# Weight ring of a two-layer mixture-of-experts trunk: single-slot transfers for the first eight experts, and norm rows loaded as 2 KB pieces and spread by products with ones

## The chip, the cores and the metric

The kernel runs on one core of a Trainium2 chip. The metric is the device time of one execution in microseconds (us), as the median of several runs; a profile of one execution gives the trace.

## The reference, cut to what matters

Two layers, each an attention block ("mixing") followed by a routed feed-forward block over 32 experts. 256 tokens of width 1024; each token goes to 2 experts, and every expert's three matrices (w1 and w3 together 4 MB, w2 2 MB, in float32) are read once per layer. Two norms per layer have a scale row g and an offset row b.

```python
h = layer_norm(x, ln_in_g, ln_in_b)
for l in range(DEPTH):                                   # 2
    mix = mixing_sublayer(h, ...)
    h = layer_norm(DEEPNORM_ALPHA * h + mix, ln1_g[l], ln1_b[l])
    ffn = hierarchical_moe(h, ...)                       # sum over chosen experts of
                                                         # gate * (silu(x @ w1[e]) * (x @ w3[e])) @ w2[e]
    h = layer_norm(DEEPNORM_ALPHA * h + ffn, ln2_g[l], ln2_b[l])
```

## The kernel before, in words

**The ring of weight slots.** All large weights pass through 1 MB slots (128 partitions x 2048 floats). `Ring` (L141) holds them as tiles of two slots and, some, of one. `jobs` (L270 to L332) lists every transfer in the order of use, with its size of one or two slots. `fill` (L180) hands the next job to a place that is free: a job of two slots needs both halves of one tile, and a job of one slot takes a lone slot first (`fits`, L171). `free` (L197) returns slots when the last matmul that reads them stands in the program. This happens while the program is built, so it fixes which transfer waits for which matmul. SP issues all these transfers on one queue, strictly in the order of the list: a transfer whose slot is still being read stops those behind it. During the experts there are 22 slots: eight tiles of two, and six lone slots.

**Experts.** `up_parts` and `down_parts` (L112, L117) say in how many pieces an expert's up weights (w1 and w3) and down weights (w2) come. Before, with `FINE = 6`, experts 0 to 5 bring their up weights in four pieces of one slot, experts 0 to 3 their down weights in two; the others come in pieces of two slots, up to the last two experts. Experts are worked off in 16 pairs i (L1513). For each pair TensorE does `up_proj` of its first expert (L1394, 32 matmuls), the down products `y_part` of the pair before (L1418, py then px), `up_proj` of its second expert, and `combine` of the pair before into four accumulators (L1430); then `scatter` (L1377, written to px), the transposes T of `glu` (L1227) and, for every second i, a `gather` (L1338). TensorE's order is written by hand (`manual_schedule`, L1512). py, px, T and ph are single PSUM banks.

**The norm rows.** The residual x*g + b of the norm before is added in two steps: `next(residual)` at i = 2 and i = 3 (L1533 to L1537). Two lone jobs of the list after pair 2, "gb" and "x", take the two halves of one tile. `gb_rows` (L265) loads the 8 KB row of g and b into "gb", read 128 times so that each partition has it: 1 MB. `residual_ffn` (L1305) scales it by ALPHA on ScalarE (L1309), computes x*g + b in "x" on GpSimd (L1313 to L1316) and at i = 3 adds it to the accumulators with four matmuls (L1320), after which both slots are freed. In the last layer one more 1 MB job "gb" stands at the end of the list (L331), for the output norm (L1564 to L1578).

Of the kernel before, what the change touches and what calls it, by code (L numbers as in the profile page):

```python
# [9 lines left out]
F32 = mybir.dt.float32  # L10
I32 = mybir.dt.int32
AF = mybir.ActivationFunctionType
# [3 lines left out]
L, S, D = 2, 256, 1024  # L16
# [6 lines left out]
ALPHA = (2 * L) ** 0.25  # L23
# [1 line left out]
NEG = -1e30  # L25
F32R = mybir.dt.float32r
SCRATCH = 1024
LIT, FINE = 3, 6
RING, PRE, LATE, EARLY, LATER = 4, 2, 6, 1, 4
STAGE, GT = 4, 2  # L30
ORDER = (2, 3, 0, 1)
# [80 lines left out]
def up_parts(e):  # L112

    return 4 if e < FINE or e >= NE - 2 else 2


def down_parts(e):  # L117

    return 2 if e < FINE - 2 else 1


def rsqrt(nc, pool, v, n):
# [81 lines left out]
def program(tc, I, out):  # L204
    nc = tc.nc
# [10 lines left out]
    def bcast(src, n):  # L216
        return bass.AP(tensor=src.tensor, offset=src.offset, ap=[[0, 128], [1, n]])
# [30 lines left out]
    ones = const.tile([128, 128], F32, name="ones")  # L248
# [13 lines left out]
                                  bass.AP(tensor=src.tensor, offset=src.offset + at + m * i, ap=[[n, 128], [1, m]]))  # L262
        return job

    def gb_rows(i):  # L265
        def job(t):
            nc.sync.dma_start(t, bcast(I["lnrows"][i], 2 * D))
        return job

    jobs = []  # L270
    for l in range(L):
        at = 0
        for key, size in mixing_plan():
            jobs.append(((l, *key), whole(wmix[l], at, size, 2 if key == ("m",) else 1), 2))
            at += 128 * size

        def up(e):

            flat = wup[l, e].rearrange("p k s f -> p (k s f)")
            parts = up_parts(e)  # L280
            n = 8192 // parts

            def job(i):
                return lambda t: nc.sync.dma_start(t[:, :n], flat[:, n * i:n * i + n])
            return [((l, "up", e, i), job(i), 4 // parts) for i in range(parts)]

        def down(e):
            flat = wdown[l, e].rearrange("p a j f -> p (a j f)")
            parts = down_parts(e)
            n = 4096 // parts  # L290

            def job(i):
                return lambda t: nc.sync.dma_start(t[:, :n], flat[:, n * i:n * i + n])
            return [((l, "w2", e, i), job(i), 2 // parts) for i in range(parts)]

        def last(es):

            held = []

            def rows(t, e, j):  # L300
                nc.sync.dma_start(t.rearrange("p (a j f) -> p a j f", a=2, j=4)[:, :, 2 * j:2 * j + 2],
                                  wdown[l, e][:, :, 2 * j:2 * j + 2])

            def first(t):
                held.append(t)
                rows(t, es[0], 0)

            def second(t):
                rows(t, es[1], 0)
                rows(held[0], es[0], 1)  # L310
                rows(t, es[1], 1)

            return [((l, "w2", e, 0), job, 2) for e, job in zip(es, (first, second))]

        n = NE // 2
        for i in range(n):
            if i in APART:
                jobs += [job for both in zip(up(2 * i), up(2 * i + 1)) for job in both]
            else:
                jobs += up(2 * i)  # L320
                jobs += down(2 * i - 2) + down(2 * i - 1) + up(2 * i + 1)
            if i == n - 2:
                jobs += down(2 * i) + down(2 * i + 1)
            if i == n - 1:
                jobs += last((2 * i, 2 * i + 1))
            if i == 2:
                jobs += [((l, "gb"), gb_rows(1 + 2 * l), 1), ((l, "x"), lambda t: None, 1)]
            if i == 5:
                jobs += [((l, "over", 0), lambda t: None, 2), ((l, "over", 1), lambda t: None, 1)]
        if l == L - 1:  # L330
            jobs += [((l, "gb"), gb_rows(2 + 2 * l), 1)]  # L331
    jobs = [(key, size, job) for key, job, size in jobs]  # L332
    early = {l: next(j for j in jobs if j[0] == (l, "up", 0, 3)) for l in range(L)}
    ring = Ring([j for j in jobs if j not in early.values()], nc.sync)
# [798 lines left out]
    def experts(l, lg, logits, split, late, c2, acc, two_parts):  # L1133
        nonlocal h
        p1 = c2.enter_context(pool_(name=f"moe{l}", bufs=1))
        wkp = c2.enter_context(pool_(name=f"wk{l}", bufs=1, space=PS, side="right"))
# [161 lines left out]
        def affine_T(xg, px, k0):  # L1298
# [3 lines left out]
                last = nc.vector.tensor_scalar(xg[:, k0 + k], px[:, k], g, b, op0=OP.mult, op1=OP.add)  # L1302
            return last

        def residual_ffn():  # L1305

            gb = ring[(l, "gb")].rearrange("p (j a d) -> p j a d", j=2, a=2)
            x = ring[(l, "x")].rearrange("p (t a d) -> p t a d", t=2, a=2)
            nc.scalar.activation(gb, gb, AF.Copy, scale=ALPHA)  # L1309
            for t in range(2):  # L1310
                xv = ring[(l, "x")][:, D * t:D * t + D]
                xv = xv.rearrange("q (p k) -> q k p", k=8) if l == L - 1 else xv.rearrange("q (k p) -> q k p", k=8)
                nc.gpsimd.tensor_tensor(xv, two_parts[0][:, t].bitcast(F32), two_parts[1][:, t].bitcast(F32), op=OP.add)  # L1313
                for a in range(2):
                    nc.gpsimd.tensor_tensor(x[:, t, a], x[:, t, a], gb[:, 0, a], op=OP.mult)
                    nc.gpsimd.tensor_tensor(x[:, t, a], x[:, t, a], gb[:, 1, a], op=OP.add)  # L1316
            yield
            for t in range(2):
                for a in range(2):
                    nc.tensor.matmul(acc[t][a], ident, x[:, t, a], start=False, stop=False, skip_group_check=True)  # L1320
            ring.free((l, "gb"), (l, "x"))
            yield
# [189 lines left out]
        with tc.manual_schedule(engines={mybir.EngineType.PE}):  # L1512
            for i in range(n - 1):  # L1513
                if i:
                    hs = up(i, 0)
                    if i - 1 in APART:
                        down_both(i - 1)
                    else:
                        for a in range(2):
                            y_part(i - 1, a)  # L1520
                    glu(i, 0, hs)
                    hs = up(i, 1)
                if i % 2:
                    q = (i + 1) // 2
                    Dm[q] = p1.tile([128, 2, 4 * C], F32R, name="Dm")
                    placed(q, 0, 1)
                Dg = (gated_both if i + 1 in APART else gated)(i + 1)
                if i:
                    if i - 1 in APART:
                        combine_both(i - 1)  # L1530
                    else:
                        combine(i - 1, *every)
                if i == 2:  # L1533
                    residual = residual_ffn()
                    next(residual)
                if i == 3:
                    next(residual)  # L1537
                scatter(i + 1, Dg)
                if i % 2:
                    for _ in gather(q):  # L1540
                        pass
                if i:
                    glu(i, 1, hs)
                if 4 <= i < 7:
                    found = next(listing)
                if i == 7:
                    overflow(*found)
                    ring.free((l, "over", 0), (l, "over", 1))
            for a in range(2):
                y_part(n - 2, a)  # L1550
            hs = evacuated(up_both(n - 1))
            combine(n - 2, *every)
            glu_both(n - 1, hs)
            down_both(n - 1)
            combine_both(n - 1)
            if l < L - 1:
                warm(wkp.tile([128, 128], F32, name="py"), 16)
        ms = moments(sts)
        h = rows()
        if l < L - 1:  # L1560
            for t in range(2):
                norm(t, acc[t], ms[t])
        else:
            gb = ring[(l, "gb")].rearrange("p (j a d) -> p j a d", j=2, a=2)  # L1564
            for t, (mean, y, nm) in enumerate(ms):
                less = small.tile([128, 1], F32, name="less")
                nc.vector.tensor_scalar(less, mean, -1.0, None, op0=OP.mult)
                for a in range(2):
                    x = halves(t)[a]
                    if t < a:  # L1570
                        nc.vector.scalar_tensor_tensor(x, acc[t][a], mean, gb[:, 0, a], op0=OP.subtract, op1=OP.mult)
                    else:
                        nc.scalar.activation(x, acc[t][a], AF.Identity, bias=less)
                        nc.gpsimd.tensor_tensor(x, x, gb[:, 0, a], op=OP.mult)
            for t, (mean, y, nm) in enumerate(ms):
                for a in range(2):
                    x = halves(t)[a]
                    nc.vector.scalar_tensor_tensor(x, x, y, gb[:, 1, a], op0=OP.mult, op1=OP.add)  # L1578
                    (nc.scalar if a else nc.sync).dma_start(out[128 * t:128 * t + 128, 512 * a:512 * a + 512], x)
# [5 lines left out]
    for l in range(L):  # L1585
        experts(l, *mixing(l))
# [57 lines left out]
```

## Time and profile before

| what | value |
|---|---|
| median of 3 runs | 1424.08 us (1423.87 to 1425.05) |
| the profiled execution | 1425.94 us, its span 1424.3 us |
| TensorE matmul busy | 1346.2 us (95% of the span) |
| VectorE, ScalarE, GpSimd busy | 579.0, 435.1, 86.6 us |
| moved by DMA | 488.69 MB |
| mean granted TensorE clock | 0.983 |

Layer 0 is mixing up to about 270 us and experts up to about 704 us; layer 1 is mixing up to about 974 us and experts up to about 1408 us. Busy shares are averages over stages with different limits: the DMA engines are near full only in the experts, where TensorE is near full as well, so what a change is worth is read from the waits in that stage.

### The profile page before, as it was taken

To read this page: it belongs to the slowest core of one execution; us is meant where nothing else is said; L and a number is where in the kernel's file an instruction comes from. 1 tells how busy PE (TensorE), PEld (TensorE's weight loads), DVE (VectorE), ACT (ScalarE), POOL (GpSimd) and SP (SyncE) were. 2 spreads that over 40 slices of the span, in tenths; PEclk is the share of its full clock that TensorE was granted. 3 is DMA by queue.
4 is the path that set the end of the run, shared out by engine and by line. 5 is a ranking of instruction groups with operands and counts; after the bars stand their busy time and mean duration, and the time that the engine had idled before them with its cause. 6 is when DMAs were issued, how large, how long until landed. Compare 5 with 4: busy or idle time off the path is not lost. (4 is left out here: it accounts for less than half of the span.)

```text
span 1424.3 us, 19771 instructions
## 1 busy us (share of the span) xinstructions
PE 1346.2 (95%) x8004; PEld 832.7 (58%) x8008; DVE 579.0 (41%) x1387; ACT 435.1 (31%) x906; POOL 86.6 (6%) x83
## 2 busy tenths in 40 slices
PE   8999999899999999989789999998999999999893
PEld 8999999543443443434379999984443434434331
DVE  6767777621221221212267676865211212112113
ACT  5556555321111111111145665543211111111111
POOL 2000030130000000000100000301300000000001
PEclk9999999999999999999999999999999999999998
DMA  9433577699999999999963337777999999999995
GB/s 387 189 119 134 214 318 300 252 398 420 427 433 424 429 429 429 431 428 427 425 257 126 119 127 301 308 282 292 390 429 430 430 425 429 430 428 431 428 425 222
DMA packets 46832, 488.69 MB, mean 343 GB/s; under 512 B 4880, under 2 KB 8464, under 8 KB 12816
## 3 DMA queue, kind: packets, MB, share of 16 engines
q1 hardware_dynamic: 46016, 486.25, 82.4%
q8 instruction: 65, 1.06, 0.3%
q10 hardware_dynamic: 720, 1.12, 0.2%
q14 instruction: 31, 0.25, 0.0%
HBM read 486.31 MB, written 1.05 MB: 342 GB/s over the span
## 5 line engine op out<-in xcount | busy, mean ns | idle before, releaser
L1394 PE MATMUL ph<-wslot,xg 128*64 128x512 f32 x1792 | 396.9, 595 | 2.6 <-ACTq L1236 2.6
L1394 PEld LDWEIGHTS ph<-wslot,xg 128*64 128x64 f32 x1792 | 123.7, 137 | 235.1 <-issue 231.6
L479 DVE TENSOR_TENSOR split<-wslot,split 128x512 fp32r<-128x512 f32 (+1 forms) x272 | 192.6, 719 | 96.1 <-ACT split L478 62.7
L478 ACT ACTIVATE split<-wslot 128x512 fp32r<-128x512 f32 (+2 forms) x276 | 168.8, 616 | 140.7 <-PE mm L510 120.2
L508 PE MATMUL mm<-hThi,split 128*128 128x256 f32 x704 | 202.5, 288 | 0.0
L510 PE MATMUL mm<-hThi,split 128*128 128x256 f32 x704 | 197.7, 281 | 0.3
L509 PE MATMUL mm<-hTlo,split 128*128 128x256 f32 x704 | 196.9, 280 | 0.0
L1220 ACT ACTIVATE hs<-ph 128x512 f32<-128x512 f32 x60 | 35.9, 598 | 404.9 <-PE ph L1394 373.1
L1422 DVE SCALAR_TENSOR_TENSOR ys<-py,gate,ys 128x512 fp32r<-128x512 f32 x28 | 21.0, 750 | 286.1 <-ACT ys L1421 286.1
L508 PEld LDWEIGHTS mm<-hThi,split 128*128 128x128 f32 x704 | 132.5, 188 | 3.7 <-ACT split L478 1.3
L510 PEld LDWEIGHTS mm<-hThi,split 128*128 128x128 f32 x704 | 132.3, 188 | 2.5 <-DVE split L479 2.3
L509 PEld LDWEIGHTS mm<-hTlo,split 128*128 128x128 f32 x704 | 132.5, 188 | 0.5 <-issue 0.5
L1418 PE MATMUL py<-wslot,gT 128*64 128x512 f32 x448 | 113.4, 614 | 9.9 <-DMA wslot<-in_down_dram 9.4
L1418 PE MATMUL px<-wslot,gT 128*64 128x512 f32 x448 | 107.8, 592 | 0.0
L1380 DVE TENSOR_SCALAR DT<-px 128x256 fp32r<-128x256 f32 x30 | 12.7, 424 | 218.2 <-PE px L1377 218.2
L1418 PEld LDWEIGHTS py<-wslot,gT 128*64 128x64 f32 x448 | 36.0, 141 | 80.6 <-issue 75.7
L1418 PEld LDWEIGHTS px<-wslot,gT 128*64 128x64 f32 x448 | 36.3, 137 | 62.5 <-issue 62.5
L1430 PE MATMUL acc<-ys,DT 128*128 128x512 f32 x224 | 59.7, 408 | 0.0
L1430 PEld LDWEIGHTS acc<-ys,DT 128*128 128x128 f32 x224 | 39.9, 188 | 30.3 <-issue 22.8
L1422 DVE SCALAR_TENSOR_TENSOR ys<-px,gate,ys 128x512 fp32r<-128x512 f32 x28 | 21.0, 751 | 75.5 <-ACT ys L1421 75.5
L1421 ACT ACTIVATE ys<-py,gate 128x512 fp32r<-128x512 f32 x28 | 19.3, 688 | 102.2 <-PE py L1418 102.2
L1421 ACT ACTIVATE ys<-px,gate 128x512 fp32r<-128x512 f32 x28 | 19.3, 688 | 77.3 <-PE px L1418 77.3
(330 smaller groups left out, 1802.4 us busy)
## 6 DMA issues: line engine op xcount, KB each, us to landing
wslot<-in_up_dram SPq DMA_DIRECT2D x96, 2048.0 KB, 17.9
wslot<-in_down_dram SPq DMA_DIRECT2D x52, 2048.0 KB, 18.9
wslot<-in_wmix_dram SPq DMA_DIRECT2D x32, 2048.0 KB, 8.7
wslot<-in_up_dram SPq DMA_DIRECT2D x64, 1024.0 KB, 14.2
wslot<-in_down_dram SPq DMA_DIRECT2D x24, 1024.0 KB, 10.9
wslot<-in_wmix_dram SPq DMA_DIRECT2D x4, 832.0 KB, 12.9
wslot<-in_lnrows_dram SPq DMA_DIRECT2D x3, 1024.0 KB, 15.4
wslot<-in_wmix_dram SPq DMA_DIRECT2D x2, 1040.0 KB, 11.5
```

The source lines that it names most:

```text
L478: nc.scalar.activation(hi, w, AF.Copy)
L479: engine.tensor_tensor(lo, w, hi.bitcast(F32), op=OP.subtract)
L508: nc.tensor.matmul(ps, st[0], mv[0], start=start, stop=False)
L509: nc.tensor.matmul(ps, st[0], mv[1], start=False, stop=False)
L510: nc.tensor.matmul(ps, st[1], mv[0], start=False, stop=stop)
L1220: nc.scalar.activation(hs, hps.rearrange("q (p j) -> q j p", j=4), AF.Copy)
L1380: nc.vector.tensor_scalar(DT, pd, 0.0, None, op0=OP.is_gt)
L1394: nc.tensor.matmul(ph[C * s:C * s + C], x[:, k, c0:c0 + C], w[:, k % part, s], start=k == 0, stop=k == 7)
L1418: nc.tensor.matmul(py[C * e:C * e + C], gTs[i, e][:, j], w[:, 0 if parts == 2 else a, j], start=j == 0, stop=j == 3)
L1421: nc.scalar.activation(ys[0], py, AF.Copy, scale=gate)
L1422: nc.vector.scalar_tensor_tensor(ys[1], py, gate, ys[0].bitcast(F32), op0=OP.mult, op1=OP.subtract)
L1430: nc.tensor.matmul(acc[t][a], st[i]["DT"][:, t], y, start=False, stop=False, skip_group_check=True)
```

## The change

`FINE` is 8, and `down_parts` uses the same bound: the up weights of experts 6 and 7 come in four pieces instead of two, the down weights of experts 4 to 7 in two instead of one, 8 transfers more per layer for the same bytes. The three 1 MB loads of norm rows become four loads of 512 floats each (2 KB, 8 KB together) into partitions 0, 32, 64 and 96 of the slot "x", and a new function `spread` copies them to all partitions: for each quarter a product of one row of ones (1 x 128) with the row (1 x 512) into py or px, and an ACTIVATE that writes it, scaled, into "gb". It stands at i = 2 of both layers. For the output norm a pair of jobs "gb2" and "x2" stands after pair 9 of the last layer instead of the job at the list's end, spread at i = 11; "gb2" is held until the end.

```diff
-LIT, FINE = 3, 6
+LIT, FINE = 3, 8
...
-    return 2 if e < FINE - 2 else 1
+    return 2 if e < FINE else 1
...
-    def gb_rows(i):
+    def rows_of(i):
+
         def job(t):
-            nc.sync.dma_start(t, bcast(I["lnrows"][i], 2 * D))
+            for j in range(4):
+                nc.sync.dma_start(t[32 * j:32 * j + 1, 0:512], I["lnrows"][i, 512 * j:512 * j + 512])
         return job
...
-                jobs += [((l, "gb"), gb_rows(1 + 2 * l), 1), ((l, "x"), lambda t: None, 1)]
+                jobs += [((l, "gb"), lambda t: None, 1), ((l, "x"), rows_of(1 + 2 * l), 1)]
...
-        if l == L - 1:
-            jobs += [((l, "gb"), gb_rows(2 + 2 * l), 1)]
+            if i == 9 and l == L - 1:
+                jobs += [((l, "gb2"), lambda t: None, 1), ((l, "x2"), rows_of(2 + 2 * l), 1)]
...
+        def spread(key, rows, scale):
+
+            for j in range(4):
+                ps = wkp.tile([128, 512], F32, name=("py", "px")[j % 2])
+                p = slice(32 * j, 32 * j + 1)
+                nc.tensor.matmul(ps, ones[p], ring[(l, rows)][p, 0:512], start=True, stop=True)
+                nc.scalar.activation(ring[(l, key)][:, 512 * j:512 * j + 512], ps, AF.Copy, scale=scale)
+
         def residual_ffn():
 
+            spread("gb", "x", ALPHA)
             gb = ring[(l, "gb")].rearrange("p (j a d) -> p j a d", j=2, a=2)
             x = ring[(l, "x")].rearrange("p (t a d) -> p t a d", t=2, a=2)
-            nc.scalar.activation(gb, gb, AF.Copy, scale=ALPHA)
...
+                if i == 11 and l == L - 1:
+                    spread("gb2", "x2", 1.0)
+                    ring.free((l, "x2"))
...
-            gb = ring[(l, "gb")].rearrange("p (j a d) -> p j a d", j=2, a=2)
+            gb = ring[(l, "gb2")].rearrange("p (j a d) -> p j a d", j=2, a=2)
```

The transfers of experts 5 to 7 on SP's queue in layer 0, before (in_up is up weights, in_down is down weights; 128x4096 fills two slots; the slot tiles' numbers are kept):

```order
L284 DMA wslot0_78<-in_up_dram 128x2048 x2
L267 DMA wslot1_182<-in_lnrows_dram 128x2048
L284 DMA wslot2_190<-in_up_dram 128x4096
L284 DMA wslot5_2100<-in_up_dram 128x4096
L293 DMA wslot6_2101<-in_down_dram 128x4096
L293 DMA wslot7_2102<-in_down_dram 128x4096
L284 DMA wslot3_191<-in_up_dram 128x4096
L284 DMA wslot4_194<-in_up_dram 128x4096
```

And now, in the changed kernel's line numbers:

```order
L286 DMA wslot0_78<-in_up_dram 128x2048 x2
L269 DMA wslot1_182<-in_lnrows_dram 1x512 x4
L286 DMA wslot_2815<-in_up_dram 128x2048
L286 DMA wslot5_2100<-in_up_dram 128x2048
L286 DMA wslot2_190<-in_up_dram 128x2048 x2
L295 DMA wslot5_2100<-in_down_dram 128x2048
L295 DMA wslot6_2101<-in_down_dram 128x2048 x2
L295 DMA wslot9_3070<-in_down_dram 128x2048
L286 DMA wslot10_3071<-in_up_dram 128x2048
L286 DMA wslot11_3072<-in_up_dram 128x2048
L286 DMA wslot12_3073<-in_up_dram 128x2048
L286 DMA wslot7_2102<-in_up_dram 128x2048
```

The up weights of experts 6 and 7 and the down weights of 4 and 5 are cut to single slots, and lone slots (2815, wslot9 to wslot12) are used once more. Further on in the same queue, from the down weights of expert 10 to those of expert 13, before:

```order
L293 DMA wslot1_182<-in_down_dram 128x4096
L293 DMA wslot0_78<-in_down_dram 128x4096
L284 DMA wslot2_190<-in_up_dram 128x4096
L284 DMA wslot5_2100<-in_up_dram 128x4096
L284 DMA wslot6_2101<-in_up_dram 128x4096
L284 DMA wslot3_191<-in_up_dram 128x4096
L293 DMA wslot4_194<-in_down_dram 128x4096
L293 DMA wslot1_182<-in_down_dram 128x4096
```

And now:

```order
L295 DMA wslot1_182<-in_down_dram 128x4096
L295 DMA wslot3_191<-in_down_dram 128x4096
L286 DMA wslot4_194<-in_up_dram 128x4096
L286 DMA wslot7_2102<-in_up_dram 128x4096
L286 DMA wslot0_78<-in_up_dram 128x4096
L286 DMA wslot5_2100<-in_up_dram 128x4096
L295 DMA wslot6_2101<-in_down_dram 128x4096
L295 DMA wslot1_182<-in_down_dram 128x4096
```

Tiles between have other numbers, but here nothing moved against its release: the down weights of expert 13 take, as before, the tile (wslot1) that those of expert 10 leave. On TensorE, at the end of i = 2 in layer 0, before:

```order
L1394 MATMUL ph<-wslot_78,xg 64x512 x8
L1430 MATMUL acc_3006<-ys,DT 128x512 x2
L1430 MATMUL acc_3007<-ys,DT 128x512 x2
L1430 MATMUL acc_3008<-ys,DT 128x512 x2
L1430 MATMUL acc_3009<-ys,DT 128x512 x2
L1377 MATMUL px<-cp,Dg 128x128 x2
L1227 MATMUL T<-cp,hs 128x128 x4
```

And now:

```order
L1404 MATMUL ph<-wslot_78,xg 64x512 x8
L1440 MATMUL acc_3006<-ys,DT 128x512 x2
L1440 MATMUL acc_3007<-ys,DT 128x512 x2
L1440 MATMUL acc_3008<-ys,DT 128x512 x2
L1440 MATMUL acc_3009<-ys,DT 128x512 x2
L1312 MATMUL py<-wslot_182,ones 128x512
L1312 MATMUL px<-wslot_182,ones 128x512
L1312 MATMUL py<-wslot_182,ones 128x512
L1312 MATMUL px<-wslot_182,ones 128x512
L1387 MATMUL px<-cp,Dg 128x128 x2
L1229 MATMUL T<-cp,hs 128x128 x4
```

The four products of `spread` stand ahead of the scatter's transposes, which write px as well.

## Rows read from the trace of the kernel before

**Rows 1.** The page's slices: 40 equal ones of the span, GB/s moved.

```profile
GB/s 387 189 119 134 214 318 300 252 398 420 427 433 424 429 429 429 431 428 427 425 257 126 119 127 301 308 282 292 390 429 430 430 425 429 430 428 431 428 425 222
```

**Rows 2.** Chain that ended last, pieces in time: start us, us, what.

```profile
1321.32 33.84 DMA wslot<-in_down_dram
...
1355.18 29.51 DMA wslot<-in_up_dram
...
1384.75 19.65 DMA wslot<-in_down_dram
...
1406.39 0.02 issue
```

**Rows 3.** TensorE's waits, 600 to 705 us: us, times, longest.

```profile
PE py L1418 <- DMA wslot<-in_down_dram: 5.1, 2, 3.9
```

**Rows 4.** TensorE's timeline: start us, us, instructions [idle before].

```profile
274.87 7.07 PE L1453 MATMUL ph<-wslot,xg 128*32 128x512 f32 x64
...
1383.45 4.83 PE L1453 MATMUL ph<-wslot,xg 128*32 128x512 f32 x36
...
1394.56 1.91 PE L1453 MATMUL ph<-wslot,xg 128*32 128x512 f32 x12 [1.38 <-DMA wslot<-in_up_dram]
```

**Rows 5.** Line L267: duration ns min/median/max, first and last start us.

```profile
L267 SPq DMA_DIRECT2D wslot<-in_lnrows_dram x3: 327/328/4590, 289.4 to 1387.2; - x3
```

**Rows 6.** Stretches: us, then PE PEld DVE ACT POOL busy, PEclk, DMA share, GB/s.

```profile
316.00:318.00 2.00, 2.00 (x12) 0.72 (x10) 0.00 (x0) 0.46 (x1) 2.00 (x3) 1.00 0.71 303
318.00:320.00 2.00, 2.00 (x12) 0.63 (x10) 0.00 (x0) 0.67 (x1) 2.00 (x2) 1.00 0.04 16
320.00:322.00 2.00, 2.00 (x12) 0.66 (x10) 0.75 (x1) 0.01 (x1) 1.56 (x2) 1.00 0.92 238
1020.00:1022.00 2.00, 2.00 (x12) 0.62 (x10) 0.00 (x0) 0.28 (x1) 2.00 (x3) 1.00 0.65 279
1022.00:1024.00 2.00, 2.00 (x12) 0.72 (x10) 0.13 (x1) 0.69 (x1) 2.00 (x2) 1.00 0.04 16
320.00:436.00 116.00, 112.48 (x550) 47.83 (x547) 25.03 (x58) 17.49 (x34) 1.56 (x2) 1.00 1.00 426
```

**Rows 7.** Line L293 at 319 us: its one transfer, landing, SP's wait.

```profile
L293 SPq DMA_DIRECT2D wslot<-in_down_dram x1: 327/327/327, 319.3 to 319.3; - x1
...
DMA to landing us min/median/max: 7.8/7.8/7.8
...
SPq L293 <- PE py L1418: 18.3, 1, 18.3
```

**Rows 8.** The same line at 436 us (down weights of expert 13, layer 0).

```profile
L293 SPq DMA_DIRECT2D wslot<-in_down_dram x1: 328/328/328, 435.8 to 435.8; - x1
...
DMA to landing us min/median/max: 9.2/9.2/9.2
...
SPq L293 <- PE px L1418: 6.5, 1, 6.5
```

**Rows 9.** The same line at 1140 us (the same transfer, layer 1).

```profile
L293 SPq DMA_DIRECT2D wslot<-in_down_dram x1: 328/328/328, 1139.7 to 1139.7; - x1
...
DMA to landing us min/median/max: 9.4/9.4/9.4
```

**Rows 10.** TensorE's timeline about the scatter of i = 2 and the residual.

```profile
332.19 0.38 PE L1377 MATMUL px<-cp,Dg 128*128 128x128 f32 x2
...
356.39 3.59 PE L1320 MATMUL acc<-wslot,cp 128*128 128x512 f32 x8
```

**Rows 11.** Lines L1320 and L1220: duration ns min/median/max, first and last start us.

```profile
L1320 PE MATMUL acc<-wslot,cp x16: 590/592/592, 356.4 to 1063.2; 128*128 128x512 f32 x16
...
L1220 ACT ACTIVATE hs<-ph x60: 597/598/599, 282.0 to 1396.5; 128x512 f32<-128x512 f32 x60
```

**Rows 12.** GpSimd's timeline: start us, us, instructions.

```profile
290.40 4.70 POOL L1313 TENSOR_TENSOR wslot<-hi,lo 128x1024 f32<-128x1024 f32 x2 [22.95 <-PE ph L1394]
...
319.05 2.52 POOL L1316 TENSOR_TENSOR wslot<-wslot 128x512 f32<-128x512 f32 x2
```

## Prediction

> **What bounds the kernel now.** I read the page's slices first, then the chain, then the waits and the transfers one by one. The slices show two kinds of stage. In the experts the DMA engines move 420 to 433 GB/s without a break, in the attention stages far less [rows 1]. The chain says what ends each expert stage: at its end it runs through three transfers, each released by the one before or by a matmul, and then the last products [rows 2]. So a layer's experts end when their last weights land. TensorE is hardly behind: it waits for down weights near the end of the layer only, 5.1 us in two places of layer 0 [rows 3], and in layer 1 the last pair's up products take from 1383.45 to 1396.47 us, 13.0 us against 7.1 us where nothing is late, so 5.9 us of waiting [rows 4].
>
> The question is therefore what sets the landing of the last weights. From some point on, the queue is never empty, and everything behind that point comes at the DMA rate: the point where a transfer is issued latest against the queue in front of it decides. Two places must be found: holes in the DMA's work, and transfers that barely escape one.
>
> A hole there is, in both layers, at the third pair: the DMA share falls to 0.71, 0.04 and 0.92 in three stretches of 2 us, which is 0.58 + 1.92 + 0.16 = 2.7 us of idling, and 0.70 + 1.92 = 2.6 us in layer 1 [rows 6]. It is SP's: the down weights of expert 5 need a whole tile, and SP waited 18.3 us for py's matmuls to leave one half of it. Issued into an empty queue, this transfer took **7.8 us** to land [rows 7]. That is the bare time of 2 MB, 4.9 us of moving and 2.9 us around it. So a transfer keeps the queue unbroken only when the one before lands 2.9 us or more after its issue.
>
> Behind the hole the share is 1.00 to 436 us, with TensorE busy 112.5 of 116 us [rows 6]: there TensorE makes room just fast enough. The transfer that comes nearest to another hole is that of expert 13's down weights. SP waits 6.5 us for px's matmuls to leave its tile, and it lands 9.2 us after its issue in layer 0 and 9.4 us in layer 1 [rows 8, 9]. It is thus only **1.4 and 1.6 us** from coming late.
>
> **The change part by part.** *Smaller norm rows.* Two of the three 1 MB loads stand in the middle of the expert stages, at 289 us and in layer 1's like place [rows 5]. At 430 GB/s [rows 1] each takes 1.05 MB / 430 = 2.4 us of the queue. The third stands behind the last weights, at 1387.2 us [rows 5], and delays none: worth nothing. The four 2 KB loads move next to nothing.
>
> *Single slots for experts 4 to 7.* Bytes are the same. The down weights of expert 5 no longer need a whole tile and may use lone slots that stood empty; they wait for expert 3's up weights, used by 302 us, and not for py at 319 us. This fills the hole: 2.7 and 2.6 us. The eight more issues a layer cost SP 0.33 us each [rows 5], under 3 us spread over a time in which SP waited 18.3 us in one piece [rows 7].
>
> Together the queue gets ahead by 2.4 + 2.7 = 5.1 us in layer 0 and 5.0 us in layer 1. But room does not come earlier. The transfers from expert 10's last up weights on wait for the same matmuls as before, in the old order. The down weights of expert 13 cannot land before their release and 7.8 us more. If TensorE kept its times, their landing could come forward by 1.4 and 1.6 us only, and the rest of the lead would turn into a new hole ahead of them.
>
> *The products of `spread`.* TensorE does not keep its times. At i = 2 four products come between combine and scatter, in a stretch where TensorE is the one that makes room. The scatter starts at 332.19 us now [rows 10]. Before it, the first product takes 0.59 us, and then four copies go through ScalarE one after another, since the third and fourth product need the banks that the first two copies empty, and the scatter needs px after the fourth copy. A copy of 128x512 out of PSUM takes 0.60 us [rows 11]. With five hand-overs between engines of some 0.03 us, near the 0.02 us of the chain's [rows 2], the delay is 0.59 + 4 x 0.60 + 0.15 = **3.1 us**. From below it is bounded by the products' own issue, (3.59 - 0.59) / 7 = 0.43 us each [rows 10], 1.7 us in all; from above by a chain in which each product waits for the copy before, 4 x (0.59 + 0.60 + 0.06) = 5.0 us. I take 3.1 us because the two banks allow the overlap and the copy, not the product, is the longer step.
>
> Every release behind it comes 3.1 us later, expert 13's tile among them. Landing of its down weights: 3.1 - 1.4 = 1.7 us later than now in layer 0, 3.1 - 1.6 = 1.5 us later in layer 1. Behind this point the queue is unbroken as now, so the last weights land as much later.
>
> *The residual.* GpSimd now starts after the spread, at some 335 us and not at 290 us. It needs 4.7 us for its two sums and eight steps of 1.26 us [rows 12], so it ends near 350 us. The four matmuls that add it stand at 356.4 us [rows 10], then at 359.5 us. Covered by 9 us; without the cover it would delay the release of two slots.
>
> *The output norm's spread at i = 11 of layer 1.* TensorE loses two copies and two products there, 0.59 + 0.60 + 0.60 + 0.59 + 0.1 = 2.5 us. This stands far behind expert 13, where the queue is full, and is hidden by the 5.9 us that TensorE waits at the last pair [rows 4]; with the 3.1 us from i = 2 it is 5.6 us, of which the later landing gives back 1.5 us. If the weights landed 5 us earlier this cover would be gone, and some 5 us of the gain with it. The slot "gb2" keeps to the end is a lone one, which transfers of two slots cannot use.
>
> **The sum.** 1.7 + 1.5 = 3.2 us slower. The profiled execution took 1425.94 us, 1424.3 us of it span; it would take 1429.1 us. The median is 1.9 us below it, so 1424.08 + 3.2 = **1427.3 us**. With the bounds of the delay: 2 x 1.7 - 3.0 = 0.4 us to 2 x 5.0 - 3.0 = 7.0 us, 1424.5 to 1431.1 us.
>
> **The rivals.** *The lead survives.* If expert 13's transfers have more reserve than I read (another transfer order, room made earlier), the 5 us of each layer reach its end: 1424.1 - 10.1 = 1414.0 us. For it: the layer's end is made of transfers alone [rows 2], and bytes go. Against it: the 6.5 us that SP waits for px ahead of this very transfer [rows 8], a wait that no freed byte shortens. It decides from the point where the reserve is over the delay of spread by what is saved. In layer 1 the cover of 5.9 us would cut it by a few us. Chance 0.17.
>
> *A shorter bare time.* The hole's transfer was issued at 319.3 us, and the DMA idled to about 320.2 us (share 0.92 of the next stretch) [rows 6, 7]: 0.9 us of the 7.8 us is getting started. If a queue that is still draining hides this, a transfer comes late only below 6.9 us, the reserves are 2.3 and 2.5 us, and the sum is 2 x 3.1 - 4.8 = 1.4 us: 1425.5 us. Against it: in the hole the queue had only just run dry when the transfer was issued, so the data of a landing was over some 2 us before it. Chance 0.15. The Trainium skill, "DMA: Bandwidth & Descriptors", section "Anatomy of one DMA", gives a fit of about 2.0 us and bytes over 436 GB/s for GpSimd's path: 6.8 us for 2 MB, by which the sum would be 2 x 3.1 - 5.0 = 1.2 us. The trace's 7.8 us on SP's path differs, and I go by it.
>
> *Nothing reaches the end.* The delay of spread is near 1.7 us, or is made up before 436 us: 1424.1 to 1424.5 us. For it: TensorE idles 3.5 of 116 us behind the hole [rows 6]. Against it: those waits follow TensorE's own products, so they move with it. Chance 0.10.
>
> **How the numbers follow.** The forecast, that spread's delay outweighs the reserve, has 0.58, with a range of its own of 1424.5 to 1431.1 us. A measurement tells 0.2% from no change, 2.8 us here. The forecast is over that when the delay is above 2.9 us, which I give 0.7 within it. Slower: 0.58 x 0.7 = 0.41. Same: the other 0.17 of it, 0.15 and 0.10, so 0.42. Faster: 0.17. The range that holds 8 in 10 takes in the two small cases and most of the forecast's own bounds, and leaves out the surviving lead: 1422.5 to 1430.5 us.
>
> **What would show it.** Right, if the DMA share stays at 1.00 from 316 to 322 us; if the scatter of i = 2 starts about 3.1 us after the first product of spread; if new holes stand between 365 and 446 us; and if expert 13's down weights land 7.8 us after their issue. Wrong, if that transfer lands well over 7.8 us after its issue, or if the last weights of a layer land earlier than now.

## Result: slower by 0.95%, 14.3 us at the median

The changed kernel took 1438.27 us, median of 4 runs (1436.28 to 1439.97), beside 1423.97 us of the kernel before: ratio 1.0095, interval 1.0082 to 1.0108 (the ratios given here differ by up to 0.1% from the quotient of the two medians beside them). The forecast was 1427.3 us, its range up to 1430.5 us: the sign of the likeliest case was right, its size far too small.

The profiled execution is the quickest of the four, 1436.28 us with a span of 1434.7 us; that of the kernel before was some 2 us above its median. So the two traces differ by 10.4 us of span, the medians by 14.3 us.

The page's slices after, GB/s [rows 1 have the line before]:

```profile
GB/s 385 188 118 133 218 318 307 260 424 426 349 406 399 429 428 430 430 429 426 424 263 127 118 124 313 306 283 297 426 399 358 408 418 430 428 428 430 429 423 201
```

The slices with the hole of the third pair, the 9th and the 29th, went up from 398 and 390 to 424 and 426 GB/s, and others behind them fell instead: 349, 406, 399 in layer 0, 399, 358, 408, 418 in layer 1. From there on the rate is full again, to the layer's end. The same stretch of layer 0 in pieces (us, length, PEclk, DMA share, GB/s), the kernel before:

```profile
280.00:340.00 60.00, 1.00 0.96 404
340.00:400.00 60.00, 1.00 1.01 431
400.00:460.00 60.00, 1.00 1.00 427
460.00:600.00 140.00, 1.00 1.01 429
```

and the changed kernel:

```profile
280.00:340.00 60.00, 0.97 1.01 424
340.00:400.00 60.00, 1.00 0.92 381
400.00:460.00 60.00, 1.00 0.97 397
460.00:600.00 140.00, 0.99 1.01 429
```

From these rows one sum is made again and again below. To 460 us the kernel before moved 60 x (404 + 431 + 427) = 75.7 MB, the changed one 72.1 MB: 3.6 MB less, 8.4 us at 429 GB/s. The changed kernel has 1.05 MB (2.4 us) less to move by then, so its queue is **5.9 us late**, and stays so: behind 460 us both run at 429. I call this the lateness of the queue.

TensorE's lateness I read at the scatter of i = 6, near 446 us, against the first scatter of the layer. The timeline of the kernel before (start us, us, instructions):

```profile
281.87 0.44 PE L1377 MATMUL T<-cp,Dg 128*128 128x128 f32 x2
...
445.32 0.38 PE L1377 MATMUL px<-cp,Dg 128*128 128x128 f32 x2
```

and after:

```profile
281.63 0.44 PE L1387 MATMUL T<-cp,Dg 128*128 128x128 f32 x2
...
450.83 0.38 PE L1387 MATMUL px<-cp,Dg 128*128 128x128 f32 x2
```

169.20 us against 163.45 us: TensorE is **5.75 us late**. It has all of it by i = 3. Where it comes from stands in TensorE's timeline after, about spread:

```profile
332.00 0.69 PE L1312 MATMUL py<-wslot,ones 1*128 1x512 f32 x1
332.01 0.69 PE L1312 MATMUL px<-wslot,ones 1*128 1x512 f32 x1
332.53 0.59 PE L1312 MATMUL py<-wslot,ones 1*128 1x512 f32 x1
332.54 0.59 PE L1312 MATMUL px<-wslot,ones 1*128 1x512 f32 x1
333.81 0.69 PE L1312 MATMUL py<-wslot,ones 1*128 1x512 f32 x1 [0.68 <-ACT wslot L1313]
...
334.83 0.59 PE L1312 MATMUL px<-wslot,ones 1*128 1x512 f32 x1
336.11 0.69 PE L1387 MATMUL px<-cp,Dg 128*128 128x128 f32 x2 [0.69 <-ACT wslot L1313]
336.59 1.06 PE L1229 MATMUL T<-cp,hs 128*128 128x128 f32 x4
337.58 7.93 PE L1404 MATMUL ph<-wslot,xg 128*64 128x512 f32 x32
```

Each of the four products is two records here. The first two run side by side and take 1.1 us together, the second two, started 0.5 us apart, 1.6 us, and behind each pair TensorE waits 0.7 us for a copy: 4.1 us from the first product to the scatter. And what follows is slow: the transposes take 1.06 us and the up products 7.93 us, which took 0.6 and 7.1 us before. The stretches say why (us, length, PE busy, PEclk, DMA share, GB/s):

```profile
334.00:336.00 2.00, 1.42 (x4) 0.98 1.00 426
336.00:338.00 2.00, 1.89 (x8) 0.50 1.01 434
338.00:340.00 2.00, 2.00 (x8) 0.67 0.95 401
340.00:342.00 2.00, 2.00 (x12) 1.00 1.01 422
```

The granted clock fell to 0.50, the lower level of 1.2 GHz, behind the two waits, and came back near 340 us. 5.75 - 4.1 = some 1.6 us are lost to it: from the scatter to the next y_part it is 9.2 us (336.11 to 345.34), and was 7.7 us before (332.19 to 339.86). In layer 1 TensorE loses 5.9 us in the same way, with the same two waits and the clock at 0.50 from 1046 to 1048 us.

### The profile page after: what moved, and what is told of

The parts are those of the page before. It is cut to its first block, busy times and chain, and to the rows that moved or that the text cites. A ratio compares the mean times of both kernels' runs of the same rounds, so it can differ in the third digit from the quotient of the medians.

```text
span 1434.7 us, 19888 instructions
## 1 busy us (share of the span) xinstructions
PE 1356.3 (95%) x8032; PEld 832.3 (58%) x8032; DVE 579.5 (40%) x1387; ACT 437.9 (31%) x916; POOL 87.3 (6%) x83
## 3 DMA queue, kind: packets, MB, share of 16 engines
q8 instruction: 65, 1.06, 0.3%
q10 hardware_dynamic: 720, 1.12, 0.2%
HBM read 483.18 MB, written 1.05 MB: 338 GB/s over the span
```

## The experiments

Theory A, formed from these traces: what TensorE loses up to 446 us reaches the layer's end whole, one for one; of what it gains there only as much reaches the end as the queue has a lead (what filled holes and fewer bytes give), so that a gain is the smaller of the two. The rivals: B, the smaller transfers or their order cost the time; C, the lead would survive if TensorE kept its times; D, the output norm's spread in layer 1; E and F as the expectations have them. Each ratio is to the kernel before on the same chip (medians 1424.58, 1424.88 and 1426.09 us for the three groups of four: single slots to output norm; late residual to halves; products early to the list).

**1. One part alone, two runs; one part left out, two runs.** The single slots alone, in the kernel before:

```diff
-LIT, FINE = 3, 6
+LIT, FINE = 3, 8
...
-    return 2 if e < FINE - 2 else 1
+    return 2 if e < FINE else 1
```

> The single slots alone: experts 4 to 7 in single-slot transfers, the norms' rows still loaded as 1 MB, no products. Theory A (the end of a layer follows TensorE's times at experts 10 to 13, and what spread costs TensorE, 5.7 us a layer, reaches the end nearly whole): TensorE keeps its times here, the hole at 316 to 322 us is filled, and the lead is given back by 446 us: 1421 to 1424.5 us. Theory B (the twice as many transfers of experts 4 to 7, or the other order in which slots come free, are what costs): 1430 us or more. Theory C (the lead would survive if TensorE kept its times): 2.7 + 2.6 us of hole saved, 1418 to 1419.5 us.

Measured 1425.47 us, ratio 0.9998 (0.9989 to 1.0008): no difference. TensorE is at 0.0 us here, and the hole is filled, a lead of 2.9 us at 340 us, which is gone by 460 us:

```profile
280.00:340.00 60.00, 1.00 1.01 425
340.00:400.00 60.00, 1.00 1.01 425
400.00:460.00 60.00, 1.00 1.00 414
```

So C falls here already. The spread alone is the changed kernel with these two lines as they were before.

> The norms' rows as 16 KB with the products alone: experts 4 and 5 keep their two-slot transfers as in the kernel before. Theory A: TensorE loses the same 5.7 us a layer at spread, and the hole at 316 to 322 us does not matter: 1434 to 1439 us, as the changed kernel. Theory B: without the smaller transfers the loss goes, and 1 MB a layer is saved: 1421 to 1428 us.

Measured 1436.97 us, 1.0078 (1.0061 to 1.0095). Within the intervals the whole loss is the spread's; B falls, with both runs.

The changed kernel without spread's products:

```diff
-                ps = wkp.tile([128, 512], F32, name=("py", "px")[j % 2])
-                p = slice(32 * j, 32 * j + 1)
-                nc.tensor.matmul(ps, ones[p], ring[(l, rows)][p, 0:512], start=True, stop=True)
-                nc.scalar.activation(ring[(l, key)][:, 512 * j:512 * j + 512], ps, AF.Copy, scale=scale)
+                to = ring[(l, key)][:, 512 * j:512 * j + 512].rearrange("p (r c) -> p r c", r=4)
+                nc.scalar.activation(to, ones[:, None, :].to_broadcast([128, 4, 128]), AF.Copy, scale=scale)
```

> The changed kernel with spread's eight products left out of TensorE: ScalarE fills the norm's rows with a constant, in as many copies, so that the loads of 16 KB, the slots and the copies stay (the norms' scale and shift are left out of the result). Theory A: TensorE keeps its old times, the queue is 5.1 us a layer ahead at first, and nearly all of that is given back in new holes before 446 us: 1419 to 1424 us. Theory B: still 1430 us or more. Theory C: the lead survives, 1413 to 1416 us. The granted clock near 336 us stays at 1.00 if its fall there is due to TensorE's waits within spread.

Measured 1427.79 us, 1.0018 (1.0008 to 1.0028), 3.8 us over the top of what I expected. The three stretches read

```profile
280.00:340.00 60.00, 1.00 1.01 425
340.00:400.00 60.00, 1.00 0.98 406
400.00:460.00 60.00, 1.00 0.99 407
```

The lead of 5 us, the saved megabyte counted, is there at 340 us and is all gone by 460 us: 74.3 MB, 3.4 us behind in bytes, 0.9 us late with the saved megabyte counted. TensorE is 0.87 us late at i = 6, its clock at 1.00 from 330 to 342 us. C falls with this run too: without spread's stall in TensorE, with 2 MB less and no hole, the time is no better than before. It is 3.2 us above the kernel before; 0.9 and 0.7 us of that are TensorE's lateness in the two layers, and what makes the rest is open: its last weights land at 1407.4 us, 3.0 us later than before [rows 2], though its bytes are hardly late.

The output norm's rows as before, 1 MB at the end of the list and no "x2":

```diff
+    def gb_rows(i):
+        def job(t):
+            nc.sync.dma_start(t, bcast(I["lnrows"][i], 2 * D))
+        return job
...
-            if i == 9 and l == L - 1:
-                jobs += [((l, "gb2"), lambda t: None, 1), ((l, "x2"), rows_of(2 + 2 * l), 1)]
+        if l == L - 1:
+            jobs += [((l, "gb2"), gb_rows(2 + 2 * l), 1)]
...
-                if i == 11 and l == L - 1:
-                    spread("gb2", "x2", 1.0)
-                    ring.free((l, "x2"))
```

> The changed kernel with the output norm's rows as in the kernel before (1 MB behind the last weights, no spread at i = 11). Theory A: nothing of it is on the path, 1436 to 1438.5 us. Theory D (the spread at i = 11 and the slot held to the end cost a part of what was lost in layer 1): 1430 to 1434 us.

Measured 1437.74 us, 1.0086 (1.0068 to 1.0104): as the changed kernel. D falls.

**2. The cost of the products by themselves, at two places.** In the kernel before, five products nobody reads, at i = 2 and, in a second run, at i = 9:

```diff
+                if i == 2:
+                    py = wkp.tile([128, 512], F32, name="py")
+                    for _ in range(5):
+                        nc.tensor.matmul(py, ident, ones[:, None, :].to_broadcast([128, 4, 128]), start=True, stop=True)
                 scatter(i + 1, Dg)
```

> The kernel before with nothing of the change, and five products of 128x512 that nobody reads ahead of the scatter of i = 2 in each layer: 5 x 1.06 = 5.3 us more for TensorE, with no wait between them. Theory A (the end of a layer moves with TensorE at 446 us): 1424.6 + 10.6 = 1435 us, 1433.5 to 1436.5 us, without any other part of the change. My prediction's own step, a reserve of 1.4 and 1.6 us, would give 1424.6 + 10.6 - 3.0 = 1432 us. If loads, slots or order made the loss: 1424 to 1427 us.

Measured 1434.73 us, 1.0052 (1.0033 to 1.0070). The products cost less than I had said (ten records, no wait):

```profile
332.32 4.45 PE L1541 MATMUL py<-ones,cp 128*128 128x512 f32 x10
```

TensorE is 4.30 us late at i = 6, and the queue, 404, 411 and 415 GB/s in the three stretches, 1.92 MB or 4.5 us. So 8.6 us for two layers by theory A, and 8.6 us is what the medians differ by (1434.73 - 1426.09). A reserve of 1.4 and 1.6 us would have left 5.6 us, which the interval (4.7 to 10.0 us) does not exclude by itself; but it would also have left the queue 2.9 us late, and it is 4.5 us late.

> The same five products ahead of the scatter of i = 9 and not of i = 2. Theory A: there the queue has a backlog of some transfers and TensorE waits for weights at the layer's end, so they cost nothing but what those waits hide badly: 1424 to 1426 us. If any work on TensorE counts wherever it stands: 1435 us.

Measured 1424.26 us, 0.9986 (0.9975 to 0.9996): not slower. The same work costs 8.6 us at i = 2 and nothing at i = 9.

**3. Spread without waits.** Two products each at the ends of i = 1 and i = 2, so that copies lie beside the next up products:

```diff
-            spread("gb", "x", ALPHA)
...
-                if i == 2:
-                    residual = residual_ffn()
-                    next(residual)
...
+                if i in (1, 2):
+                    spread("gb", "x", ALPHA, (2 * i - 2, 2 * i - 1))
+                if i == 2:
+                    residual = residual_ffn()
+                    next(residual)
```

> The changed kernel with spread in two halves of two products, each ahead of an expert's up products (i = 1 and i = 2), so that the copies lie beside 7 us of other products and TensorE has no wait within spread; the output norm's spread as it is. Theory A: TensorE loses the products alone, 4 x 1.1 = 4.4 us a layer instead of 5.7, and its clock stays at 1.00 if the waits made it fall: 1424.3 + 8.8 = 1433 us, 1432 to 1434.5 us. If the clock falls all the same, or the first half waits for its rows: 1436 to 1439 us.

Measured 1432.92 us, 1.0063 (1.0046 to 1.0080); the profiled execution is the quickest of the four, 1429.29 us. TensorE's timeline at the second half, then the clock behind it (columns as above):

```profile
332.36 0.69 PE L1312 MATMUL py<-wslot,ones 1*128 1x512 f32 x1
332.89 0.66 PE L1312 MATMUL px<-wslot,ones 1*128 1x512 f32 x1
332.90 0.59 PE L1312 MATMUL py<-wslot,ones 1*128 1x512 f32 x1
333.40 0.59 PE L1312 MATMUL px<-wslot,ones 1*128 1x512 f32 x1
333.91 7.09 PE L1403 MATMUL ph<-wslot,xg 128*64 128x512 f32 x32
```

```profile
334.00:336.00 2.00, 2.00 (x10) 1.00 0.98 418
```

No idle time, clock at 1.00, up products in 7.09 us: TensorE is 3.68 us late in place of 5.75. 2 x 3.7 = 7.4 us of the measured 8.0 are the products. So the fall of the clock goes with the waits. This run also parts the four products into two pairs; but five products in a row and without a wait (products early, 4.45 us, with 128 rows of weights) left the clock at 1.00 too.

**4. Work moved out of the stretch.** Three runs move the norm's rows (the jobs "gb" and "x", the first lines) and the residual to i = 9 and 10:

```diff
-            if i == 2:
+            if i == 7:
...
-                if i == 2:
+                if i == 9:
                     residual = residual_ffn()
                     next(residual)
-                if i == 3:
+                if i == 10:
                     next(residual)
```

> The changed kernel with the norm's rows, spread and the residual of each layer moved from i = 2 and 3 to i = 9 and 10, behind the stretch in which TensorE makes room. Theory A (a layer ends as much earlier or later as TensorE is at 446 us, as long as the queue has a lead to use): spread no longer counts, the residual's four matmuls, 3.6 us, leave the stretch too, and of the queue's lead of 5.1 us a layer 3.6 us reach the end: 1424.3 - 7.2 = 1417 us, 1415 to 1420 us. Theory E (another wait near 446 us takes over as soon as TensorE is earlier, or the work is missed at i = 9): 1422 to 1427 us.

Measured, in the changed kernel: 1419.69 us, 0.9964 (0.9952 to 0.9976), faster than both. TensorE is 3.4 us early at i = 6, the queue 3.7 us.

> The kernel before with the same move of the norm's rows (its 1 MB loads) and of the residual to i = 9 and 10. TensorE is 3.6 us earlier at 446 us as well, but the queue has the hole at 316 to 322 us and no lead: from 322 us on it moves data at full rate already, and only the order changes, with 1 MB less in front of 446 us. Theory A: the lead is the 2.4 us of that megabyte at 446 us, but it comes later in the same queue, so nothing is gained at the end: 1423 to 1425.5 us. Theory F (TensorE alone sets the end): 1417 us.

Measured, in the kernel before: 1423.24 us, 0.9986 (0.9976 to 0.9996). The number fits, the reason did not: the hole at 316 to 322 us was mostly filled here too (377 GB/s, 186 before), by the code because the jobs "gb" and "x" no longer hold a whole tile then. TensorE is 3.4 us early; at 460 us the weights are 3.8 us ahead of before, and all bytes together 1.4 us, as the 1 MB of the norm's rows, 2.4 us, is still to come.

> The single slots alone (experts 4 to 7) with the 1 MB loads, and the norm's rows and the residual moved to i = 9 and 10: no products. Theory A: the lead is the 2.6 us of the hole, and TensorE is 3.6 us earlier, so the smaller of the two reaches the end: 1424.3 - 5.2 = 1419 us, 1418 to 1421 us. Theory E: 1422 to 1427 us; theory F: 1417 us.

Measured, in the kernel with single slots alone: 1423.42 us, 0.9996 (0.9986 to 1.0005). A miss of 4 us: I had counted the hole as lead and forgotten that the moved megabyte comes behind 446 us, where every byte delays the end. By the stretches the queue has 0.6 us to the good; 3.4 - 2.4 would be 1.0. Of the rivals, F (1417 us) falls with the last two runs. E's 1422 to 1427 us fits these two by the number, but not the first run, 1419.69 us, where TensorE is as early.

**5. A version that beats both.** The changed kernel with spread in halves at i = 8 and 9, the residual's products at i = 10; then also the list of overflowing experts moved (with it the two jobs of the ring that it fills), three steps on TensorE, each behind a wait of 1.6 us for bank T:

```diff
-            if i == 5:
+            if i == 8:
...
-                if 4 <= i < 7:
+                if 7 <= i < 10:
                     found = next(listing)
-                if i == 7:
+                if i == 10:
                     overflow(*found)
```

> The changed kernel with rows and residual moved behind 446 us as in the run with the late residual, and spread in two halves ahead of up products, at the ends of i = 8 and 9; the residual's matmuls stay at i = 10. Theory A: the end is set by the queue as before, so the same 1417 to 1420 us, at best 1 to 2 us less if the fall of TensorE's clock at 527 us had cost something at the end.

Measured 1418.11 us, 0.9940 (0.9923 to 0.9956).

> The run before with the list of the overflowing experts (three steps on TensorE, each with a wait of 1.6 us for bank T) moved from i = 4 to 6 to i = 7 to 9 and the overflow from i = 7 to 10. Theory A: TensorE is another 5 us earlier at 446 us, of which the queue's lead that is left, 5.1 - 3.9 = 1.2 us a layer, reaches the end: 2.4 us less than the run before, 1415 to 1417 us. If TensorE alone set it: 1407 to 1409 us. If the later slots of the overflow cost room: no gain, 1418 to 1422 us.

Measured **1415.93 us**, 0.9926 (0.9910 to 0.9943): 10.2 us under the kernel before and 2.2 us under the run before it, as expected (four times each, 1415.37 to 1416.58 and 1416.61 to 1419.34 us). Its scatters and its stretches:

```profile
280.73 0.44 PE L1386 MATMUL T<-cp,Dg 128*128 128x128 f32 x2
...
436.99 0.38 PE L1386 MATMUL px<-cp,Dg 128*128 128x128 f32 x2
```

```profile
280.00:340.00 60.00, 1.00 1.01 425
340.00:400.00 60.00, 1.00 1.01 430
400.00:460.00 60.00, 1.00 1.01 429
```

TensorE is 7.2 us early, the queue never pauses and is 3.1 us ahead in bytes, 5.5 us with the saved megabyte. So the lead is now the smaller one, and 2 x 5.5 = 11 us is near the 10.2 us measured. TensorE alone would have given 14 us and more.

All runs in one table, layer 0, in us against the kernel before (late is +; the queue's number counts the megabyte as saved where it is never loaded, and as still to come in the two runs marked):

| run | TensorE at i = 6 | queue at 460 us | median less its kernel before |
|---|---|---|---|
| single slots alone | 0.0 | -0.3 | +0.9 |
| products late (i = 9) | 0.0 | -0.3 | -1.8 |
| no products | +0.9 | +0.9 | +3.2 |
| spread in halves | +3.7 | +3.6 | +8.0 |
| products early (i = 2) | +4.3 | +4.5 | +8.6 |
| output norm loaded | +5.8 | +5.7 | +13.2 |
| the changed kernel | +5.75 | +5.9 | +14.3 |
| spread alone | +5.9 | +6.1 | +12.4 |
| late residual | -3.4 | -3.7 | -5.2 |
| the same in halves | -3.4 | -3.4 | -8.0 |
| before, late residual | -3.4 | -1.4 (1 MB to come) | -1.6 |
| slots, late residual | -3.4 | -0.6 (1 MB to come) | -1.5 |
| and the list late | -7.2 | -5.5 | -10.2 |

The first two columns agree within 0.3 us wherever TensorE sets the queue, and differ only where the lead has run out (the last run) or a megabyte was put off. In layer 1 TensorE's numbers repeat within 0.2 us, and the queue's lie within 0.8 us of them in the same runs. The last column is about twice the second, give or take 3 us. It is the rougher one, as executions of one kernel differ by several us. Within the traces, from the first scatter of layer 0 to the end of the span, the changed kernel takes 10.6 us longer than the kernel before (1434.7 - 281.63 against 1424.3 - 281.87), spread alone 12.2, products early 8.3, halves 6.1 and no products 2.2 us; late residual takes 8.5 and the list late 9.1 us less. All thirteen lie within 2.1 us of twice the second column.

## Why the prediction was wrong, step by step

**Right.** The hole at 316 to 322 us is filled:

```profile
316.00:318.00 2.00, 2.00 (x12) 0.62 (x10) 0.00 (x0) 0.19 (x1) 0.00 (x0) 1.00 1.03 426
318.00:320.00 2.00, 2.00 (x12) 0.67 (x10) 0.25 (x1) 0.69 (x1) 0.00 (x0) 1.00 1.01 418
```

where [rows 6] had shares of 0.71 and 0.04. The lead of 5 us a layer exists (no products, at 340 us). It does not survive: the rate falls in the slices from 359 to 466 us, and behind them it is full. The landing of expert 13's weights, the last of the signs I had named, can't be read here: the trace of the changed kernel has no landing times. GpSimd is no matter: its part of the residual ends at 346.3 us, and the products that need it start at 361.9 us. The output norm's spread costs nothing that can be measured (run with the output norm loaded).

**Wrong, the larger term: the delay of spread, 3.1 us forecast, 5.0 us as its upper bound, 5.75 and 5.9 us measured.** Two things, and only both together pass the bound. "The first product takes 0.59 us" took one record for one product; [rows 10] had it: x8 for the residual's four matmuls. A product takes 1.1 us (the two records of one by itself), so the copies do not hide the third and fourth, and stall and products make 4.1 us. The second is the fall of the clock behind the two waits, 1.6 us, which was no term of the sum. The clock stands at 1.00 in this stretch of the kernel before [rows 6], and I did not ask what spread's own waits would do to it, though the same trace has it at 0.50 from 622 to 624 us, behind a wait.

**Wrong, the smaller term: the reserve, 1.4 and 1.6 us forecast, none measured.** The step was "a transfer keeps the queue unbroken only when the one before lands 2.9 us or more after its issue", from a transfer issued into an empty queue [rows 7]. Two runs contradict it. With single slots alone TensorE keeps its times, so by the prediction expert 13's weights could land 1.4 and 1.6 us earlier, a gain of 3.0 us; the ratio's interval allows a gain of 1.6 us at most, and issued at 436.2 us they land 9.8 us later, at 446.0 us, where it was 445.0 us before. With the products early TensorE is 4.30 us late and the queue 4.5 us, and they land at 440.3 + 9.9 = 450.2 us. In that run they follow the transfer before them by 4.8 us, so nothing broke there; the queue had broken ahead of them, as at these up weights:

```profile
L284 SPq DMA_DIRECT2D wslot<-in_up_dram x1: 328/328/328, 430.0 to 430.0; - x1
...
DMA to landing us min/median/max: 10.4/10.4/10.4
```

The transfer in front of them landed at 417.2 + 16.7 = 433.9 us, 3.9 us after this issue, yet they land 6.5 us behind it, where 2 MB at 429 GB/s take 4.9 us. So it was not one transfer that decided. Single slots alone has more such, the first in the line of the down weights at 398.7 us:

```profile
L293 SPq DMA_DIRECT2D wslot<-in_down_dram x1: 327/327/327, 398.7 to 398.7; - x1
...
DMA to landing us min/median/max: 10.8/10.8/10.8
```

The transfer in front landed at 395.3 + 8.3 = 403.6 us, 4.9 us after this issue, well over 2.9 us, yet this one lands 5.9 us behind it. The next, issued at 405.5 us, lands 10.1 us later and 6.1 us behind the one in front, and the queue moves 381 and 352 GB/s in the two stretches of 4 us about 408 us, though a transfer was outstanding all the time. A longer bare time does not explain it either: the transfer at 395.3 us itself,

```profile
L284 SPq DMA_DIRECT2D wslot<-in_up_dram x1: 328/328/328, 395.3 to 395.3; - x1
...
DMA to landing us min/median/max: 8.3/8.3/8.3
```

broke nothing: the one in front of it landed at 387.1 + 11.6 = 398.7 us, 3.4 us after its issue, and it follows by 4.9 us. So the step that failed is the reserve read from one transfer and one bare time. There was none, as the 4.5 us show; why some transfers come late that are issued 4 to 5 us before the one in front lands, and others do not, stays open.

The Trainium skill, "DMA: Bandwidth & Descriptors", section "Anatomy of one DMA", has some 2.0 us and bytes over 436 GB/s for GpSimd's path, an estimate of 6.8 us for 2 MB; by that the reserve would have been larger still. The measurement decides.

**The sum with the right terms:** 5.75 + 5.9 = 11.7 us, 1424.1 + 11.7 = 1435.7 us, beside 1438.3 us measured (the profiled execution: 1436.28). In the profiled execution nothing is left over. Its last weights land at

```profile
1395.93 19.69 DMA wslot<-in_down_dram
```

1415.62 us, or 1133.99 us behind the first scatter of layer 0, where it was 1404.40 [rows 2] less 281.87 = 1122.53 us: 11.5 us later. The 2.6 us between that sum and the median, and some 2 us in the run without products, are not settled. The clock falls more than once where TensorE waits for late weights, as behind a wait of 2.05 us at 568.8 us of the changed kernel, and these differ from run to run; that they make the rest was not tried.

**The rivals.** The lead does survive as soon as TensorE has been taken out of the way: 1415.93 us in the last run, beside the 1414.0 us of that rival. Its condition was read rightly (room made earlier), only the change itself does not bring it. The shorter bare time had larger reserves, 2.3 and 2.5 us, and falls with the reserve, though a landing under 7.8 us does occur: 7.2 us in products early, for the transfer issued at 341.0 us. That nothing reaches the end is refuted by the 5.75 us of TensorE and the 5.9 us of the queue.

## What to carry to other kernels

Find the stretch in which an engine makes room for the transfers, and judge each edit by what it does to that engine before the last point where the queue runs thin: the same five products cost 8.6 us there and nothing 190 us later. Holes filled and bytes saved are a lead, not a gain; they become one only when the engine that frees the slots is moved forward too, and the gain is then the smaller of the two. When products, copies and banks alternate, place them in pairs ahead of long work, so that the engine never waits.

## What was not expected of the hardware

- A float32 product with 512 columns is two records of TensorE. With one row of weights it took 1.12 us by itself (halves, 306.05 us); with 128 rows it took 0.89 us in a row of five (4.45 us). Two products of one row, with the row in another partition, ran side by side in 1.1 us at 332.0 us of the changed kernel, but one behind the other in 2.2 us in halves, at 306.05 and 307.11 us.
- Behind four such products with two waits of 0.7 us the granted clock stood at 0.50 for some 4 us; the same products in pairs with no wait left it at 1.00.
- With one transfer of 2 MB still in front of it, a transfer of 2 MB landed 8.3 to 10.8 us after its issue in one run (single slots alone); into an empty queue it had taken 7.8 us [rows 7].
